# A diffusion-transformer layer on one core: 500 drawn plans for the list scheduler, and the last features' conditioning on TensorE

## The chip, the cores and the metric

One core of a Trainium2 chip runs the whole layer in one launch. The core has TensorE (matrix products into PSUM), VectorE, ScalarE and GpSimd, which work on SBUF and partly on PSUM, and a queue that issues DMAs (SyncE); ScalarE issues a few DMAs of its own. The profile calls them PE, DVE, ACT, POOL and SP; PEld is PE's weight load. The metric is the device time of one execution in microseconds, taken as the median of several runs.

## The reference

The layer takes latent tokens `x` (256 x 2048), context tokens `ctx` (256 x 2048) and two conditioning vectors, `c` for the latents and `c_ctx` for the context, all in float32. In short:

```python
sh1, sc1, g1, sh2, sc2, g2 = ada_mods(c, w_ada, b_ada)       # silu(c) @ w_ada + b_ada, w_ada is 2048 x 12288
csh1, csc1, *_ = ada_mods(c_ctx, w_ada, b_ada)
q, k, v = mixer_qkv(x * (1 + sc1) + sh1, w_in)               # w_in is 2048 x 3072; two head groups, rotary
qc, kc, vc = mixer_qkv(ctx * (1 + csc1) + csh1, w_in)        # keys and values of the context
heads = concat(window_attention(...), global_attention(...)) # latent queries on latent and context keys
x = layer_norm(2**0.25 * x + g1 * (heads @ w_out))           # w_out is 2048 x 2048
u = x * (1 + sc2) + sh2
x = layer_norm(2**0.25 * x + g2 * ((silu(u @ w_gate) * (u @ w_up)) @ w_down))   # hidden width 5632
```

With 256 + 256 tokens nearly every weight is read once, and the conditioning (`w_ada`) has as many bytes as two of the large weights.

## The kernel before, in words

**Arithmetic.** Products keep float32 accuracy by splitting both operands into a high part `hi` and a rest `lo` and adding three products of a faster type (`mm3`, lines 278 to 280, one line for each). ScalarE makes `hi` (a copy with a cast, line 519 in the planned part, 268 behind it), VectorE makes `lo` (a subtraction, lines 522 and 269). Every matmul of this kind has 128 x 128 weights and 512 moving columns.

**Features in groups.** The 16 blocks of 128 features (`k` 0 to 15) of `x` and `ctx` come in five groups: k 0; k 1; k 2 and 3; k 4 to 7; k 8 to 15 (`GROUPS`). For each group the kernel first needs shift and scale of these features. It loads the columns of `w_ada`, multiplies them with silu(c) and silu(c_ctx) (held as columns in `cs`), adds the bias (`shc`, `scc`), flips the tokens' features with TensorE (line 738), modulates them on ScalarE (744), splits them (`uh`, `ul`, lines 751 and 754), and multiplies them with the rows of `w_in` that belong to the group. A block of 512 columns of `w_in` is one "block"; four blocks hold queries (latents only, 2 row tiles), two hold keys and values (4 row tiles). The sums of a block live in SBUF (`qacc`, `kvacc`) from one group to the next.

**Two ways to sum the conditioning.** `flow_columns` does it on TensorE: four 32-column strips of the array take four k at a time (line 570, eight matmuls for a step of two 1 MB loads where four feature blocks are done together), ScalarE copies the bank (599), and TensorE adds the four strips and turns the row into columns with small products against `sel` (604). `flow_vector_columns` does it on VectorE: each load is multiplied by a scalar per partition and added to a running sum (632, 634), then the sum is turned and reduced (658, 661), and TensorE adds the partition groups with `fold` (685). The list `VECTOR_K` says which k take the second way: 12, that is the features k 12 to 15.

**Between groups.** From group index `SEED_G` on, a PSUM bank is first filled with the sums so far by ScalarE (`flow_seed`, line 534), the products are added on top, and ScalarE copies the bank back (803). Before that index the bank starts empty and VectorE adds it to the sums (805).

**What sets the order.** Everything up to the first feed-forward products is written as steps of a `Flow`: each has an engine, an assumed duration in ns, the steps that it follows, the buffers it takes and gives back, and an earliest time (`since`). `forward` runs a list schedule over five engines (SP stands for the DMA issue and the transfer's bandwidth): at each moment an engine starts, of its steps that are ready, the one with the lowest rank whose buffers are free. `backward` works out how late each step could start; these times become the ranks of the next round. `run` makes eight rounds, keeps the plan that ends first, and issues the instructions of each step in its order. The hardware queues then follow that order, each engine on its own, with semaphores between them: the assumed durations don't delay anything on the chip, they only decide the order.

The steps include 56 fillers (`WARM`, `warm_step`, matmul at line 1237 through `warm`), a chain of small matmuls on the identity. They depend only on each other and carry the highest first rank, so that the planner puts them where it sees nothing else for TensorE.

**After the plan.** A few first products of the feed-forward part are written by hand (lines 1549 to 1591), and the rest, some 740 us, is a plain program that the diff doesn't touch: `w_gate` and `w_up` products (`project`), the gate, a transposition through DRAM, `w_down`, and the second normalisation.

Of the kernel before, what the change touches and what calls it, by code (L numbers as in the profile page):

```python
# [47 lines left out]
VECTOR_K = (12,)  # L48
EARLY_WARM = 5
COLD = 3  # L50
SLACK = 2500
# [6 lines left out]
SEED_G = 3  # L58
# [16 lines left out]
class Flow:  # L75
# [8 lines left out]
    ROUNDS = 8  # L84

# [98 lines left out]

    def run(self):
        best, end = None, math.inf
        for _ in range(self.ROUNDS):
            order, last = self.forward()
            if not order:
                break  # L190
            if last < end:
                best, end = [(s, s.start, [b.pool for b in s.take]) for s in order], last
            late = self.backward(last)
            for i, s in enumerate(self.steps):
                s.rank = (late[s], i)
        assert best, "no step can start"
        for s, s.start, pools in best:
            for b, b.pool in zip(s.take, pools):
                pass
            s.fn()  # L200
# [3 lines left out]
def dit_layer(ctx: ExitStack, tc: tile.TileContext, x, c, cx, c_ctx, w_ada, b_ada, w_in, q_norm_g,  # L204
# [15 lines left out]
    def wk_bank():  # L220
        return wk_ps.tile([P, NB], F32, tag="wk", name="wk")
# [119 lines left out]
    fold = main.tile([P, 32], F32, tag="fold", name="fold")  # L341
    nc.vector.reduce_sum(fold, ident.rearrange("p (a i) -> p i a", a=4), axis=AX.X)
# [94 lines left out]
    def const_tables():  # L437
        nc.gpsimd.tensor_scalar_mul(nsink, sinkb, -1.0)
        for t in range(NT):
            for g, cg, sg in ((gq, cosQ, sinQ), (gk, cosK, sinK)):  # L440
# [19 lines left out]
             {"SP": 1300.0, "PE": 5600.0, "ACT": 5000.0, "DVE": 4000.0, "POOL": 4000.0})  # L460
# [68 lines left out]
    def flow_seed(ps, src, after):  # L529


        def fn():
            ps.t, ps.seeded = acc_bank(), True
            nc.scalar.copy(ps.t, src())

        return F.add("ACT", 475, fn, after, [ps])

    def flow_products(hl, deps, ready, cols, ps, xs, first, last, prev):
# [14 lines left out]
        return F.add("PE", 688 * len(cols), fn, after, [ps] if first and not seed else [], list(hl.rooms))  # L553
# [3 lines left out]
    def flow_columns(c0, ncol, shift, scale, ats, at):  # L557
# [18 lines left out]
        for g in range(ns):  # L576
            F.at = ats[g]
            ns1 = nk / 4 * (40 + 1.67 * width)
            if not c0:
                for i, k, m, since in ((0, 0, KD, 7200.0), (1, 0, KD // 2, 9700.0), (1, KD // 2, KD // 2, 11300.0)):  # L580
# [7 lines left out]
            if c0:  # L588
# [4 lines left out]
                prev = F.add("PE", 2 * ns1 + 420, both, [l0, l1, prev], [bank] if g == 0 else [], [r0, r1])  # L593
# [24 lines left out]
    def flow_vector_columns(c0, ncol, shift, scale, ats, at):  # L618

        width = ncol * P  # L620
        w = 2 * width
        nk = G4 * NB // w
        ns = KD // nk
        sums, last = [Buf("b4"), Buf("b4")], [None, None]

        def term(s, g, i, raw):
            if g == i == 0:
                sums[s].t = b4([P, 2 * NB], F32, "csum")
            a, src = sums[s].t[:, :w], raw.t[:, i * w : (i + 1) * w]
            k = 4 * (g * nk + i) + 2 + s  # L630
            if g == i == 0:
                nc.vector.tensor_scalar_mul(a, src, cs[:, k, None])
            else:
                nc.vector.scalar_tensor_tensor(a, src, cs[:, k, None], a, op0=ALU.mult, op1=ALU.add)  # L634

        for g in range(ns):
            F.at = ats[g * len(ats) // ns]
            raw = Buf("raw", "araw")

            def load(g=g, raw=raw):  # L640
                raw.t = pools[raw.pool].tile([P, G4 * NB], F32, tag="raw", name="raw")
                vector_load(raw.t, (c0, c0 + D), width, g)

            ld = F.add("SP", dma_ns(P * G4 * NB * 4, 2048), load, take=[raw])
            last_load[:] = [ld]
            for i in range(nk):
                for s in range(2):
                    last[s] = F.add("DVE", 1215, lambda s=s, g=g, i=i, raw=raw: term(s, g, i, raw), [ld, last[s]],
                                    [sums[s]] if g == i == 0 else [], [raw])
        F.at = at  # L650
        part = pa.tile([P, 2, w // 32], F32, tag="cpart", name="cpart")
        ready, ps = [], Buf("wk")
        for s in range(2):
            turned = Buf("b4")

            def turn(s=s, turned=turned):
                turned.t = b4([P, 2 * NB], F32, "cturn")[:, :w]
                nc.vector.transpose(turned.t, sums[s].t[:, :w])

            def reduce(s=s, turned=turned):  # L660
                nc.vector.reduce_sum(part[:, s, :], turned.t.rearrange("p (b j) -> p b j", j=32), axis=AX.X)

            a = F.add("DVE", 1150, turn, [last[s]], [turned], [sums[s]])
            ready.append(F.add("DVE", 1130, reduce, [a], give=[turned]))

        def gather():
            ps.t = wk_bank()
            fold_parts(ps.t, part, 2 * ncol)

        def add(i):  # L670
            pv = ps.t[:, : 4 * ncol].rearrange("p (s i j) -> p i j s", s=2, i=2)
            bs, bc = (bcol[:, k : k + ncol, None].to_broadcast([P, ncol, 2]) for k in (c0 // P, c0 // P + KD))
            if i == 0:
                nc.vector.tensor_tensor(shift, pv[:, 0], bs, op=ALU.add)
            else:
                nc.vector.scalar_tensor_tensor(scale, pv[:, 1], 1.0, bc, op0=ALU.add, op1=ALU.add)

# [1054 lines left out]
```

## Time and profile before

| | |
|---|---|
| median of 3 runs | 1137.29 us (1137.07 to 1138.73) |
| profiled execution | 1137.66 us, of which the trace spans 1135.9 |
| TensorE matmul busy | 1115.5 us, 98% |
| TensorE weight load busy | 904.2 us, 80% |
| VectorE busy | 858.8 us, 76% |
| ScalarE busy | 564.5 us, 50% |
| moved by DMA | 321.26 MB, mean 283 GB/s |
| mean granted TensorE clock | 0.995 |

How to read it: the share of busy time is a mean over stages with different limits. In about the first 140 us, when `w_ada` and the first half of `w_in` come in, the DMA engines are full. Between about 140 and 390 us (the last group, attention, the output projection) VectorE is nearly full. From about 390 us on the feed-forward products run. A matmul's row in the timeline has a start and a modelled end; neighbouring matmuls overlap in these rows, so the spacing of the starts says how long one takes, and a product of the split kind follows the one before after 0.23 us. A float32 matmul leaves two records. A wait shows as an idle time in brackets with the instruction that ended it.

### The profile page before, as it was taken

Reading aid. Unit: us, or ns where it says so; the run is one execution under the profiler, and the core shown is the slowest. Engines: PE = TensorE matmul, PEld = TensorE weight load, DVE = VectorE, ACT = ScalarE, POOL = GpSimd, SP = SyncE. Lnnn points to the kernel's source line nnn. Section 1 sums busy time; section 2 is a strip of 40 time slices with the busy share of each in tenths; the row PEclk is TensorE's granted clock in tenths of the full one; section 3 lists DMA queues with packets and bytes.
Section 4 is the critical chain, followed back from the end, with each engine's and each line's share of the span. In section 5 each row is a group of like instructions: output and inputs, shape, how many; then the busy total and the mean of one; then the engine's idle time right before and its main releaser. Section 6 shows DMA issues by size and latency. Waiting matters only on the chain.

```text
span 1135.9 us, 14202 instructions
## 1 busy us (share of the span) xinstructions
PE 1115.5 (98%) x5293; PEld 904.2 (80%) x5293; DVE 858.8 (76%) x1074; ACT 564.5 (50%) x815; POOL 40.1 (4%) x82
## 2 busy tenths in 40 slices
PE   8999999999999999999999999999999999999995
PEld 6766878777888788888888888888888888888884
DVE  4768999999998997767677566767766787676556
ACT  3444584977774355445464444454444443333341
POOL 1000040101100000000000000000000000000000
PEclk9999999999999999999999999999999999999998
DMA  9999999687999789999866776777777989877631
GB/s 299 384 384 396 382 353 371 217 299 227 348 340 388 280 296 316 321 313 319 302 204 211 251 223 224 244 246 249 221 245 246 306 315 333 318 274 253 203 137 74
DMA packets 186413, 321.26 MB, mean 283 GB/s; under 512 B 8764, under 2 KB 51164, under 8 KB 184039
## 3 DMA queue, kind: packets, MB, share of 16 engines
q1 hardware_dynamic: 184536, 319.25, 81.7%
q10 hardware_dynamic: 1808, 1.11, 0.3%
q8 instruction: 41, 0.67, 0.2%
q14 instruction: 28, 0.23, 0.1%
HBM read 304.07 MB, written 16.25 MB: 282 GB/s over the span
## 4 chain that ended last, share of the span: by engine, by line
PE 83%; DVE 7%; DMA 6%; ACT 1%; SPq 1%; issue 1%; DVEq 0%; ACTq 0%
PE acc L278 25%; PE acc L280 25%; PE acc L279 25%; DMA raw<-in_w_in_dram 4%; PE wk L1046 2%; DVE lo L522 2%; PE wk L570 1%; SPq L496 1%; DVE csum L634 1%; ACT hi L519 1%; PE wk L403 1%; DMA lgb<-in_ln_b_dram 1%; DVE hx L1028 1%; PE wk L738 0%; PE wk L1099 0%
## 5 line engine op out<-in xcount | busy, mean ns | idle before, releaser
L269 DVE TENSOR_TENSOR lo<-raw,hi 128x1024 fp32r<-128x1024 f32 x258 | 312.4, 1220 | 176.0 <-ACT hi L268 172.4
L268 ACT CAST hi<-raw 128x1024 fp32r<-128x1024 f32 x258 | 271.3, 1055 | 349.7 <-PE acc L280 298.5
L280 PE MATMUL acc<-hi,u2l 128*128 128x512 f32 x704 | 274.1, 389 | 1.2 <-DVE u2l L1556 1.2
L279 PE MATMUL acc<-lo,u2h 128*128 128x512 f32 x704 | 274.0, 389 | 0.6 <-DVE lo L269 0.6
L278 PE MATMUL acc<-hi,u2h 128*128 128x512 f32 x704 | 274.6, 390 | 0.0
L280 PEld LDWEIGHTS acc<-hi,u2l 128*128 128x128 f32 x704 | 132.1, 188 | 29.6 <-DVE u2l L1556 2.1
L279 PEld LDWEIGHTS acc<-lo,u2h 128*128 128x128 f32 x704 | 132.2, 188 | 28.1 <-DVE lo L269 1.0
L278 PEld LDWEIGHTS acc<-hi,u2h 128*128 128x128 f32 x704 | 132.2, 188 | 28.0 <-ACT u2h L1555 0.8
L519 ACT CAST hi<-raw 128x1024 fp32r<-128x1024 f32 (+1 forms) x86 | 87.7, 1032 | 97.7 <-PE acc L280 47.2
L278 PE MATMUL acc<-hi,hTh 128*128 128x512 f32 x344 | 135.5, 394 | 0.0
L280 PE MATMUL acc<-hi,hTl 128*128 128x512 f32 x344 | 133.9, 389 | 0.0
L279 PE MATMUL acc<-lo,hTh 128*128 128x512 f32 x344 | 133.9, 389 | 0.0
L393 DVE SCALAR_TENSOR_TENSOR adav<-raw,cs,adav 128x512 f32<-128x512 f32 (+1 forms) x128 | 121.2, 947 | 15.4 <-DMA raw<-in_w_ada_dram 13.6
L522 DVE TENSOR_TENSOR lo<-raw,hi 128x1024 fp32r<-128x1024 f32 (+1 forms) x86 | 101.3, 1194 | 18.8 <-ACT hi L519 18.7
L278 PE MATMUL acc<-hi,uh 128*128 128x512 f32 x256 | 103.5, 404 | 2.7 <-ACT qacc L803 2.6
L279 PE MATMUL acc<-lo,uh 128*128 128x512 f32 x256 | 100.1, 391 | 0.1
L280 PE MATMUL acc<-hi,ul 128*128 128x512 f32 x256 | 100.1, 391 | 0.0
L279 PEld LDWEIGHTS acc<-lo,hTh 128*128 128x128 f32 x344 | 64.6, 188 | 14.4 <-issue 0.7
L278 PEld LDWEIGHTS acc<-hi,hTh 128*128 128x128 f32 x344 | 64.6, 188 | 14.1 <-issue 1.0
L280 PEld LDWEIGHTS acc<-hi,hTl 128*128 128x128 f32 x344 | 64.6, 188 | 13.5
L278 PEld LDWEIGHTS acc<-hi,uh 128*128 128x128 f32 x256 | 48.1, 188 | 19.8 <-issue 4.6
L280 PEld LDWEIGHTS acc<-hi,ul 128*128 128x128 f32 x256 | 48.0, 188 | 10.8 <-DVE ul L754 0.4
(216 smaller groups left out, 1195.0 us busy)
## 6 DMA issues: line engine op xcount, KB each, us to landing
raw<-in_w_ada_dram SPq DMA_DIRECT2D x63, 1024.0 KB, 7.8
raw<-in_w_gate_dram SPq DMA_DIRECT2D x44, 1024.0 KB, 7.0
raw<-in_w_up_dram SPq DMA_DIRECT2D x44, 1024.0 KB, 5.4
raw<-in_w_down_dram SPq DMA_DIRECT2D x44, 1024.0 KB, 5.3
raw<-in_w_ada_dram SPq DMA_DIRECT2D x66, 512.0 KB, 6.4
raw<-in_w_in_dram SPq DMA_DIRECT2D x18, 1024.0 KB, 7.3
raw<-in_w_out_dram SPq DMA_DIRECT2D x16, 1024.0 KB, 9.3
pd<-hx SPq DMA_DIRECT2D x64, 128.0 KB, 3.9
```

The source lines that it names most:

```text
L268: nc.scalar.copy(hi[:, :n], raw[:, s : s + n])
L269: nc.vector.tensor_tensor(lo[:, :n], raw[:, s : s + n], hi[:, :n].bitcast(F32), op=ALU.subtract)
L278: nc.tensor.matmul(ps, lhsT=xh, rhs=w[0], start=first, stop=False, skip_group_check=seeded)
L279: nc.tensor.matmul(ps, lhsT=xh, rhs=w[1], start=False, stop=False, skip_group_check=seeded)
L280: nc.tensor.matmul(ps, lhsT=xl, rhs=w[0], start=False, stop=last, skip_group_check=seeded)
L393: nc.vector.scalar_tensor_tensor(a[:, c : c + piece], raw[:, f : f + piece], cs[:, 4 * (g * (G4 * NB // w) + j) + 2, None], a[:, c : c + p ...
L403: nc.tensor.matmul(ps, lhsT=ones, rhs=sb[:, s : s + NB], start=True, stop=True)
L496: nc.sync.dma_start(room.t.rearrange("p (k n) -> p k n", k=nk), w[k0 * P : (k0 + nk) * P, c0 : c0 + width].rearrange("(k p) n -> p k n", p=P),
L519: nc.scalar.copy(hl.hi[:, :n], raw.t[:, s : s + n])
L522: nc.vector.tensor_tensor(hl.lo[:, :n], raw.t[:, s : s + n], hl.hi[:, :n].bitcast(F32), op=ALU.subtract)
L570: nc.tensor.matmul(bank.t[32 * j : 32 * j + 32, :width], lhsT=cs[:, 4 * k + 2 - 2 * i : 4 * k + 34 - 2 * i], rhs=raw.t[:, c * width : (c + ...
L1046: nc.tensor.matmul(o_ps.t[:, : 2 * P].rearrange("p (g q) -> p g q", q=32), lhsT=v, rhs=pv[:, k], start=k == 0, stop=k == 3)
```

## The change

Four things are edited.

1. `run` keeps its eight rounds and then draws 500 variants: it takes the ranks of the best plan so far, changes those within a random stretch of time (each third one by a random amount, or all steps of one engine by the same amount), plans forward, and keeps the result if it ends earlier. After 3 in 10 of such finds it ranks all steps anew from the backward pass and plans once more. The generator has a fixed seed, so the order is the same in every build.
2. Durations and earliest times in the plan are set to other values, named in the diff. The loads of `x` and `ctx` get an earliest time by group (`X_FROM`), and where ScalarE issues them, a step with no instruction on SP stands for their bandwidth.
3. `VECTOR_K`, `flow_vector_columns`, `fold_parts` and the table `fold` are gone: k 12 to 15 take `flow_columns` too.
4. `SEED_G` goes from 3 to 4: only the last group (k 8 to 15) is seeded.

```diff
-VECTOR_K = (12,)
+X_FROM = {1: 13000.0, 2: 22000.0}
+CAST_FROM = 16300.0
+SEED = 7
-SEED_G = 3
+SEED_G = 4
+    TRIES = 500
...
+    def plan(self):
+        order, last = self.forward()
+        if order and last <= self.end:
+            self.end, self.rank = last, [s.rank[0] for s in self.steps]
+            self.best = [(s, s.start, [b.pool for b in s.take]) for s in order]
+            return True
+        return False
+
+    def give_ranks(self, ranks):
+        for i, (s, r) in enumerate(zip(self.steps, ranks)):
+            s.rank = (r, i)
+
+    def late_ranks(self, end):
+        late = self.backward(end)
+        self.give_ranks([late[s] for s in self.steps])
...
+        draw = random.Random(SEED)
+        for _ in range(self.TRIES):
+            ranks = list(self.rank)
+            a, w, d = draw.uniform(0, self.end), draw.uniform(2e3, 4e4), draw.gauss(0, 3e3)
+            near = [i for i, r in enumerate(ranks) if a <= r <= a + w]
+            kind, e = draw.random(), draw.choice(self.ENGINES)
+            for i in near:
+                if kind < 0.6:
+                    ranks[i] += draw.gauss(0, 3e3) if draw.random() < 0.3 else 0
+                else:
+                    ranks[i] += d if self.steps[i].eng == e else 0
+            self.give_ranks(ranks)
+            if self.plan() and draw.random() < 0.3:
+                self.late_ranks(self.end)
+                self.plan()
...
-    fold = main.tile([P, 32], F32, tag="fold", name="fold")
-    nc.vector.reduce_sum(fold, ident.rearrange("p (a i) -> p i a", a=4), axis=AX.X)
...
-             {"SP": 1300.0, "PE": 5600.0, "ACT": 5000.0, "DVE": 4000.0, "POOL": 4000.0})
+             {"SP": 2300.0, "PE": 5600.0, "ACT": 5000.0, "DVE": 4000.0, "POOL": 4000.0})
...
-        return F.add("ACT", 475, fn, after, [ps])
+        return F.add("ACT", 519, fn, after, [ps])
...
-        return F.add("PE", 688 * len(cols), fn, after, [ps] if first and not seed else [], list(hl.rooms))
+        return F.add("PE", 681 * len(cols), fn, after, [ps] if first and not seed else [], list(hl.rooms))
...
-                for i, k, m, since in ((0, 0, KD, 7200.0), (1, 0, KD // 2, 9700.0), (1, KD // 2, KD // 2, 11300.0)):
+                for i, k, m, since in ((0, 0, KD, 7200.0), (1, 0, KD // 2, 9900.0), (1, KD // 2, KD // 2, 11900.0)):
...
-                prev = F.add("PE", 2 * ns1 + 420, both, [l0, l1, prev], [bank] if g == 0 else [], [r0, r1])
+                prev = F.add("PE", 1865, both, [l0, l1, prev], [bank] if g == 0 else [], [r0, r1])
...
-    def flow_vector_columns(c0, ncol, shift, scale, ats, at):
...
-    def fold_parts(ps, part, n):
...
-        columns = flow_vector_columns if k0 in VECTOR_K else flow_columns
-        copy, ready = columns(k0 * P, n, shc[:, k0 : k0 + n, :], scc[:, k0 : k0 + n, :], ats, at + 0.8 * each)
+        copy, ready = flow_columns(k0 * P, n, shc[:, k0 : k0 + n, :], scc[:, k0 : k0 + n, :], ats, at + 0.8 * each)
...
-                a = F.add(issue, 500 if issue == "ACT" else max(ns, 500), load, take=room, since=9300.0)
-                loads.append((a, -4500) if issue == "ACT" else a)
+                a = F.add(issue, 500 if issue == "ACT" else max(ns, 500), load, take=room, since=X_FROM.get(k0, 0.0))
+                loads.append(F.add("SP", ns, lambda: None, [(a, -1000)]) if issue == "ACT" else a)
...
-                piece, = flow_weights(w_in, k0, 1, b0 * NB, m * NB, ("b4",), since=14000.0 if i and g == 0 else 0.0)
+                piece, = flow_weights(w_in, k0, 1, b0 * NB, m * NB, ("b4",), since=CAST_FROM if i and g == 0 else 0.0)
...
-            s = [F.add("PE", 760, lambda i=i, f=scores: f(i), qk, [banks[i]], [*qT[gi][0], *kT[w][0]]) for i in range(2)]
+            s = [F.add("PE", 745 if i else 690, lambda i=i, f=scores: f(i), qk, [banks[i]], [*qT[gi][0], *kT[w][0]]) for i in range(2)]
...
-            v = F.add("PE", 1760, values, g, [o_ps], [pT, *kv_room[w]])
+            v = F.add("PE", 1545, values, g, [o_ps], [pT, *kv_room[w]])
...
-                last = F.add("DVE", 1215, lambda g=g, i=i, room=room: vector_sum(room.t, a, w, g, i), [ld, last], give=[room])
+                last = F.add("DVE", 1197, lambda g=g, i=i, room=room: vector_sum(room.t, a, w, g, i), [ld, last], give=[room])
...
-            outs[n, t] = F.add("DVE", 710, spread, [(a, 80)])
+            outs[n, t] = F.add("DVE", 620, spread, [(a, 80)])
...
-            a = F.add("PE", 900, fn, [(last_sum, -SLACK)], [room])
+            a = F.add("PE", 860, fn, [(last_sum, -SLACK)], [room])
```

More of the change, by code (lines that the diff above doesn't have):

```diff
@@ L1 @@
 import heapq
+import random
 import math
@@ L183, in backward @@
         return start
+    def plan(self):
[11 more added lines that the diff above has]
+        self.give_ranks([late[s] for s in self.steps])
     def run(self):
-        best, end = None, math.inf
+        self.best, self.end = None, math.inf
         for _ in range(self.ROUNDS):
@@ L190, in run @@
                 break
[L191 to L197, printed above, removed]
+            self.plan()
+            self.late_ranks(last)
+        assert self.best, "no step can start"
+        draw = random.Random(SEED)
[12 more added lines that the diff above has]
+                self.late_ranks(self.end)
+                self.plan()
+        for s, s.start, pools in self.best:
             for b, b.pool in zip(s.take, pools):
@@ L616, in flow_columns @@
         return a, [F.add("DVE", 160, lambda i=i: add(i), [b, bias_ready], give=[ps]) for i in range(2)]
-    def flow_vector_columns(c0, ncol, shift, scale, ats, at):
[L620 to L676, printed above, removed]
-        b = F.add("PE", 500, gather, ready, [ps])
-        return b, [F.add("DVE", 160, lambda i=i: add(i), [b, bias_ready], give=[ps]) for i in range(2)]
@@ L681, in fold_parts @@
-    def fold_parts(ps, part, n):
-        pv = part.rearrange("p s (j r) -> p s j r", r=4)
-        for r in range(4):
-            nc.tensor.matmul(ps[32 * r : 32 * r + 32, : pv.shape[1] * n].rearrange("p (s j) -> p s j", j=n), lhsT=fold,
-                             rhs=pv[:, :, :, r], start=True, stop=True)
     u = {}
```

## The prediction

> **What bounds the kernel now.** I read the page first: busy shares, the slices, the chain of waits.
>
> ```profile
> span 1135.9 us, 14202 instructions
> ...
> PE 1115.5 (98%) x5293; PEld 904.2 (80%) x5293; DVE 858.8 (76%) x1074; ACT 564.5 (50%) x815; POOL 40.1 (4%) x82
> ...
> DVE  4768999999998997767677566767766787676556
> ...
> DMA  9999999687999789999866776777777989877631
> ...
> PE 83%; DVE 7%; DMA 6%; ACT 1%; SPq 1%; issue 1%; DVEq 0%; ACTq 0%
> ```
>
> TensorE (PE) holds the chain. VectorE (DVE) is full from slice 6 to slice 13, about 140 to 370 us, and the DMA engines are full up to about 140 us. So the first question is whether TensorE loses anything to either there. Next the windows by stage, with TensorE's matmul records and weight loads counted:
>
> ```profile
> 28.40:145.00 116.60, 116.35 (x724) 84.15 (x722) 94.22 (x110) 56.25 (x89) 0.00 (x0) 1.00 1.05 383
> 145.00:392.00 247.00, 245.59 (x1145) 196.65 (x1145) 232.79 (x366) 165.43 (x326) 27.39 (x58) 1.00 0.90 312
> ...
> 700.00:800.00 100.00, 100.00 (x443) 82.81 (x442) 72.04 (x86) 48.47 (x55) 0.00 (x0) 1.00 0.73 238
> ```
>
> The columns are length, then busy time (and records) of PE, PEld, DVE, ACT, POOL, then clock, DMA share, GB/s. In the feed-forward stage 443 matmuls take 100 us, 226 ns each, without a gap. Busy time could still hide waits, since the ends of matmuls are modelled, so I went to starts. Two waits stand out in the list of waits of PE, and the timeline shows them and the smaller ones as starts that come later than 0.23 us after the one before:
>
> ```profile
> PE acc L278 <- ACT qacc L803: 2.6, 1, 2.6
> ...
> PE acc L280 <- DVE u2l L1556: 1.2, 1, 1.2
> ```
>
> ```profile
> 5.47 2.50 PE L1237 MATMUL wk<-ident 128*128 128x128 f32 x10
> ...
> 14.51 2.70 PE L1237 MATMUL wk<-ident 128*128 128x128 f32 x22
> 16.97 0.48 PE L278 MATMUL acc<-hi,uh 128*128 128x512 f32 x1
> ...
> 25.05 0.39 PE L280 MATMUL acc<-hi,ul 128*128 128x512 f32 x1
> 28.05 0.50 PE L278 MATMUL acc<-hi,uh 128*128 128x512 f32 x1 [2.61 <-ACT qacc L803]
> ...
> 74.95 0.40 PE L280 MATMUL acc<-hi,ul 128*128 128x512 f32 x1
> 75.48 1.06 PE L604 MATMUL wk<-sel,ada 128*128 128x4 f32 x8
> ...
> 118.64 4.62 PE L1237 MATMUL wk<-ident 128*128 128x128 f32 x40
> 123.02 0.48 PE L278 MATMUL acc<-hi,uh 128*128 128x512 f32 x1
> ...
> 264.07 0.40 PE L280 MATMUL acc<-hi,oTl 128*128 128x512 f32 x1
> 264.54 1.99 PE L1046 MATMUL wk<-pT,kvacc 128*128 128x256 f32 x8
> ...
> 390.25 0.40 PE L279 MATMUL acc<-lo,u2h 128*128 128x512 f32 x1
> 391.85 0.50 PE L280 MATMUL acc<-hi,u2l 128*128 128x512 f32 x1 [1.20 <-DVE u2l L1556]
> ```
>
> From 25.05 to 28.05 are 3.00 us where 0.23 is normal: 2.8 lost. At 75 us 0.3 is lost, at 264 us 0.24, and four more starts of this kind between 138 and 149 us, where DVE has the least room, add some 0.9: 1.4 in all for the six. With the 1.4 at 390 us (1.60 from start to start, less 0.23; the list counts from the modelled end), everything that TensorE waits for between its first product at 16.97 us and the end of the planned part is **about 5.6 us**. Between 145 and 392 us a full DVE costs TensorE almost nothing.
>
> Then there are the fillers, L1237: matmuls of the identity that the plan issues when it sees nothing else for TensorE, two records each.
>
> ```profile
> L1237 PE MATMUL wk<-ident 128*128 128x128 f32 x112 | 15.8, 293 | 0.0
> ```
>
> 112 records are 56 fillers, the constant WARM. The twenty at 118.64 us hold TensorE for 4.4 us (to 123.02), 0.22 each. The point on which my forecast rests: each filler is a step of the plan like any other, the plan is complete only with all its steps, and the diff leaves WARM at 56. A better order moves fillers; it doesn't remove them. So TensorE's time to the end of the planned part is the sum of real work, 56 fillers and true waits, and only the first and the last can change.
>
> **The change part by part.** *The last features (k 12 to 15).* DVE loses:
>
> ```profile
> L634 DVE SCALAR_TENSOR_TENSOR csum<-raw,cs,csum 128x1024 f32<-128x1024 f32 x30 | 36.4, 1273 | 0.5 <-DMA raw<-in_w_ada_dram 0.5
> ...
> L658 DVE STREAM_TRANSPOSE cturn<-csum 128x1024 f32<-128x1024 f32 x2 | 2.4, 1213 | 0.0
> ...
> L661 DVE TENSOR_REDUCE cpart<-cturn 128x32 f32<-128x1024 f32 x2 | 2.3, 1202 | 0.0
> ```
>
> 36.4 + 2.4 + 2.3 = 41.1 us, and two first products (L632) beside these. TensorE gains what flow_columns issues: four steps of eight matmuls (16 records, two loads of 1 MB each), then four small sums. The trace has both for k 8 to 11, and the fold that goes:
>
> ```profile
> 110.85 0.39 PE L280 MATMUL acc<-hi,ul 128*128 128x512 f32 x1
> 111.17 1.92 PE L570 MATMUL wk<-raw,cs 128*32 128x512 f32 x16
> 113.02 0.50 PE L278 MATMUL acc<-hi,uh 128*128 128x512 f32 x1
> 113.36 0.40 PE L279 MATMUL acc<-lo,uh 128*128 128x512 f32 x1
> ...
> 132.00 0.95 PE L604 MATMUL wk<-sel,ada 128*128 128x4 f32 x8
> 132.80 1.07 PE L738 MATMUL wk<-ident,xt 128*128 128x128 f32 x8
> ...
> 145.15 0.26 PE L685 MATMUL wk<-cpart,fold 128*32 128x16 f32 x8
> 145.52 0.50 PE L278 MATMUL acc<-hi,uh 128*128 128x512 f32 x1
> ```
>
> One step between products: 110.85 to 113.36 is 2.51, less two normal spacings of 0.23, 2.05. Four are 8.2; if they stand side by side the changes to and fro are saved, 4 x 1.85 + 0.2 = 7.6. The sums take 132.80 - 132.00 = 0.8, the fold gave back 0.4. Added to TensorE: **8.0 to 8.6; I take 8.6**, since the plan kept such steps apart for k 8 to 11. One ACT copy of the bank (0.6, by L534's copy of the same size below) joins the queue ahead of the modulation; SP issues 8 loads of 1 MB instead of 16 of 512 KB, the same bytes, and they return their rooms after two matmul steps rather than after DVE's queue.
>
> In its sentence apart: the Trainium skill, "Perfetto Trace Analysis", Identifying the Most-Contended Engine, says that matmul busy time is a poor measure and that headroom is read from the share of weight loads. By it PEld's 80% would leave a fifth free and the 8.6 would cost nothing. The 700 to 800 row stands against it: 82.81 of 100 with 443 matmuls at an even 226 ns, so the missing 17% is spacing, not room.
>
> *Seeds of group 3 (k 4 to 7).* Sixteen banks are no longer filled by ACT ahead of the products, and their sums leave by an addition on DVE instead of a copy on ACT.
>
> ```profile
> L534 ACT COPY acc<-qacc 128x512 f32<-128x512 f32 x16 | 9.2, 587 | 0.2
> ...
> L805 DVE TENSOR_TENSOR qacc<-qacc,acc 128x512 f32<-128x512 f32 x16 | 10.7, 682 | 3.6 <-PE acc L280 3.6
> ```
>
> ACT sheds 32 x 0.59 = 19 us, DVE takes 16 x 0.68 = 11; with the above DVE is still 30 us lighter. TensorE's work is the same. If DVE comes late with such an addition, a bank returns late; by the row above that is some tenths of a us, and I take zero, up to 1 kept for the range.
>
> *The planner.* The 500 draws run on the host. They, the new durations and earliest times (X_FROM, CAST_FROM, SP from 2300) change only the order, the issue of x and ctx included: for k 1 and k 2 to 3 these (0.26 + 0.52 MB; at 383 GB/s 2 us of DMA) now stand later in ACT's queue, behind casts, and no longer ahead of the weights whose landing ends the 2.8 us wait. They wait there behind whatever cast or copy stands first; what waits for them are the flips of k 1 and k 2 (k 3 with it), TensorE's products behind those. So the most that all reordering can give is the 5.6 us of waits, and where it fills them it does so with fillers taken from 118 us. I expect back the 2.8 and the 0.9 at 138 to 149 us, where DVE's sums are gone: 3.7 of the 5.6. The u2l wait comes of the order after the plan, which stays. Bounds: 5.6 regained, or nothing regained and new waits.
>
> New waits have no row in this trace. From below zero; from above each is worth the one at 25 us, 2.8, and I allow two of them at the most, with DMA at 1.05 and each step now wanting two whole loads. I take 0.5 (nearer to zero, since in the 364 us after 28 us there are only small ones and the one at 390).
>
> *Sum* against the profiled execution, 1137.66 (1135.9 span + 1.76 around it): + 8.6 - 3.7 + 0.5 = + 5.4, so 1143.1. This execution is 0.37 above the median of the runs, 1137.29, so in their terms **1142.7**.
>
> **The rivals.**
>
> *All waits go.* + 8.6 - 5.6 = + 3.0: 1140.3. For it: a search that keeps the earliest of 500 plans, with times from a trace. Against it: the plan's time is not the chip's; at 118 us it placed 4.4 us of fillers where nothing waits after.
>
> *Not slower, by fewer changes between kinds of matmul.* The first L278 after another kind starts its successor late (113.02 to 113.36 is 0.34, not 0.23), and this is in the group means:
>
> ```profile
> L278 PE MATMUL acc<-hi,uh 128*128 128x512 f32 x256 | 103.5, 404 | 2.7 <-ACT qacc L803 2.6
> L279 PE MATMUL acc<-lo,uh 128*128 128x512 f32 x256 | 100.1, 391 | 0.1
> ```
>
> 256 x 13 ns = 3.3 us, and each column step pays a further 0.1 before it. An order that halves the changes gives 1.7 to 2.0, and steps side by side lower the 8.6 to 8.0. With all waits gone: 8.0 - 5.6 - 2.0 = + 0.4, 1137.7: no change. It decides only if both happen nearly in full. To be faster, it needs work that I don't see in the diff to leave TensorE, or the fillers to cost nothing.
>
> *New waits.* The order chosen is the one that the model flatters most, and the twenty fillers that gave DMA and DVE time at 118 us now stand earlier. Two new waits of 2.8 with 2.8 of the old regained and the rest kept: 8.6 - 2.8 + 5.6 = + 11.4, 1148.7. Against it: TensorE has more of its own work before 145 us, so it is the data that get more time. In its sentence apart: the Trainium skill, "TensorE: Matmul & The Clock Gate", Part 1, says that an idle window of about 3.4 us halves the clock until a busy one has passed; a wait of that length would cost a further 1.7, an estimate from that page. The trace agrees at the start (five fillers take 2.50 at 5.47 us, eleven take 2.70 at 14.51), but the 2.8 at 25 us slowed nothing.
>
> *The draws find no better plan*, and TensorE merely gets 8.6 more with no wait regained: 1145.9. It lies within the forecast's spread.
>
> **How the numbers follow.** Forecast with its spread (1140.8 to 1147) 0.56; all waits gone, 1139.7 to 1140.8, 0.14; not slower by fewer changes 0.12; new waits (over 1147) 0.12; faster for a reason not seen here 0.06. What tells from no change is 0.2%, 2.3 us: slower means above 1139.6, faster below 1135.0. Slower 0.56 + 0.14 + 0.12 = 0.82, less 0.04 for the edge of the second case: 0.78; same 0.12 + 0.04 = 0.16; faster 0.06. The range runs from 1138.0, inside the not-slower case, to 1149.0, inside the new waits, and leaves out about 0.2; it takes in both ends of every cost above.
>
> **What would show it.** L570 with 384 records instead of 320, L604 with 32, L634, L658, L661 and L685 gone, L534 16 fewer and L805 16 more; L1237 still 112 records, now nearly all before 60 us; no wait of over 1 us at 25 us; DVE's busy time in 28 to 145 us down by over 25 us, and in 145 to 392 us little changed; the feed-forward stage the same in rate, merely later by the total. Wrong would be: fewer than 112 filler records, a wait list of PE longer than two entries beyond the start, or a first product much off 16.97 us. If the kernel is faster with TensorE's records as counted, then spacing that I took for fixed was waiting.

## The result, and the profile after

The changed kernel takes 1144.51 us (median of 4 runs, 1144.07 to 1145.23); the kernel before took 1137.18 beside it. The ratio is 1.0059 with a 95% interval of 1.0044 to 1.0074: slower by about 7 us, where 5.4 was forecast; the time lies inside the stated range. The profiled execution took 1144.55 us, of which the trace spans 1142.8, against 1135.9 before: 6.9 us to explain.

First the page after: the span, the busy shares, the slices of VectorE, the chain by engine. Lines have moved with the diff: the three products are L310 to L312 (L278 to L280 before), the column sums L600 (L570), the fillers L1196 (L1237).

```profile
span 1142.8 us, 14235 instructions
...
PE 1123.8 (98%) x5357; PEld 907.7 (79%) x5357; DVE 828.3 (72%) x1053; ACT 548.3 (48%) x784; POOL 45.8 (4%) x82
...
DVE  3764479899999897767667566766766787676556
...
PE 96%; DVE 2%; ACT 0%; DMA 0%; issue 0%; POOL 0%; DVEq 0%; ACTq 0%; POOLq 0%
```

TensorE has 64 records more (5357 for 5293: 64 column sums and 8 small ones more, 8 folds less), VectorE is 30.5 us less busy, and the chain, which was 83% TensorE, is now 96% TensorE: the change took nearly everything else off the path and lengthened the path itself. The windows by stage of the changed kernel (columns as in the prediction):

```profile
28.40:145.00 116.60, 116.60 (x732) 79.34 (x734) 66.28 (x96) 42.42 (x64) 0.00 (x0) 1.00 0.99 358
145.00:392.00 247.00, 247.00 (x1156) 201.09 (x1152) 227.29 (x356) 161.07 (x314) 31.17 (x57) 1.00 0.91 315
...
700.00:800.00 100.00, 100.00 (x443) 82.81 (x442) 69.92 (x81) 48.36 (x57) 0.00 (x0) 1.00 0.74 246
```

VectorE's 94.2 us between 28 and 145 us became 66.3. The DMA rate there fell from 383 to 358 GB/s. The feed-forward stage is the same, 443 matmuls in 100 us. So the time lies before it. Where, the timeline of TensorE says (starts and lengths; the first product is at 21.88 us, the first feed-forward product at 397.08):

```profile
6.23 5.06 PE L1196 MATMUL wk<-ident 128*128 128x128 f32 x22
...
19.95 2.17 PE L1196 MATMUL wk<-ident 128*128 128x128 f32 x18
21.88 0.48 PE L310 MATMUL acc<-hi,uh 128*128 128x512 f32 x1
...
209.37 1.33 PE L1196 MATMUL wk<-ident 128*128 128x128 f32 x10
...
397.08 0.50 PE L310 MATMUL acc<-hi,u2h 128*128 128x512 f32 x1 [1.42 <-ACT u2h L1514]
```

Before, these two starts were at 16.97 and 389.92. So 4.9 us were lost before the first product, 2.25 between the first product and the feed-forward part (375.20 for 372.95), and a net 0.3 came back behind. The last two figures are cut at a wait: the 1.42 us at 397.08 count in the 2.25, while the kernel before has its wait of 1.20 behind that mark, at 391.85. Right behind it 1.4 us come back, and about 1.1 are lost again in small pieces of the feed-forward part. Before the first product stand 43 fillers where 28 stood, and the plan put 13 more behind it, eleven of them between 209 and 246 us, in the middle of attention. The records by line, and TensorE's list of waits:

```profile
L310 PE MATMUL acc<-hi,uh 128*128 128x512 f32 x256 | 104.8, 409 | 0.0
...
L600 PE MATMUL wk<-raw,cs 128*32 128x512 f32 x192 | 23.1, 598 | 0.0
...
L1196 PE MATMUL wk<-ident 128*128 128x128 f32 x112 | 17.5, 308 | 0.0
...
L600 PE MATMUL wk<-raw,cs 128*32 128x128 f32 x128 | 4.6, 286 | 0.0
...
L634 PE MATMUL wk<-sel,ada 128*128 128x4 f32 x32 | 3.9, 237 | 0.0
...
L600 PE MATMUL wk<-raw,cs 128*32 128x256 f32 x64 | 3.9, 382 | 0.0
```

```profile
PE wk L361 <- DMA crow<-in_c_ctx_dram: 2.1, 1, 2.1
PE wk L359 <- POOL ident masks.py:199: 1.5, 1, 1.5
PE acc L310 <- ACT u2h L1514: 1.4, 1, 1.4
PE acc L311 <- DVE lo L301: 0.8, 1, 0.8
PE wk L1366 <- DVE xt L1131: 0.3, 1, 0.3
```

Still 112 filler records, and 384 of the column sums (192 + 128 + 64). The wait at 25 us and the small ones are gone; one at the first feed-forward product stays (on ScalarE's `u2h` now, 1.4, where it was VectorE's `u2l`, 1.2). Added up start to start over the planned part, the column sums take 7.0 us more, the small sums 0.7 more, the fold 0.4 less: 7.35 us of new work. The waits behind the first product fell by 4.2, from 5.6 to 1.4. What ate that: 0.8 on the wait for `crow` at the very start, 0.8 because more fillers ran in the first microseconds, where a filler takes 0.5 us, and some 1.3 on more changes between kinds of matmul (TensorE changes into products 78 times for 65, and the mean of the first of three products rose from 404 to 409 ns over 256 of them). This makes 6.05 of the 6.9 us; the other 0.85 is spread over places of some tenths each.

### The profile page after: what moved, and what is told of

Its sections match the earlier page's. It is cut to its first block, busy times and chain, and to the rows that moved or that the text cites. A ratio compares the mean times of both kernels' runs of the same rounds, so it can differ in the third digit from the quotient of the medians.

```text
span 1142.8 us, 14235 instructions
## 1 busy us (share of the span) xinstructions
PE 1123.8 (98%) x5357; PEld 907.7 (79%) x5357; DVE 828.3 (72%) x1053; ACT 548.3 (48%) x784; POOL 45.8 (4%) x82
## 4 chain that ended last, share of the span: by engine, by line
PE 96%; DVE 2%; ACT 0%; DMA 0%; issue 0%; POOL 0%; DVEq 0%; ACTq 0%; POOLq 0%
PE acc L310 28%; PE acc L311 28%; PE acc L312 28%; PE wk L600 3%; PE wk L1005 2%; PE wk L1196 1%; PE wk L310 1%; PE wk L312 1%; PE wk L697 1%; PE wk L311 1%; PE wk L433 1%; PE wk L1058 0%; DMA crow<-in_c_ctx_dram 0%; DVE xt L1600 0%; DVE xt L1596 0%; PE wk L1333 0%
## 5 line engine op out<-in xcount | busy, mean ns | idle before, releaser
L310 PE MATMUL acc<-hi,u2h 128*128 128x512 f32 x704 | 274.7, 390 | 1.4 <-ACT u2h L1514 1.4
L312 PE MATMUL acc<-hi,u2l 128*128 128x512 f32 x704 | 274.1, 389 | 0.0
L310 PEld LDWEIGHTS acc<-hi,u2h 128*128 128x128 f32 x704 | 132.2, 188 | 29.9 <-ACT u2h L1514 2.3
L311 PEld LDWEIGHTS acc<-lo,u2h 128*128 128x128 f32 x704 | 132.2, 188 | 28.4 <-DVE lo L301 1.1
L312 PEld LDWEIGHTS acc<-hi,u2l 128*128 128x128 f32 x704 | 132.1, 188 | 27.8 <-DVE u2l L1515 0.6
L310 PE MATMUL acc<-hi,hTh 128*128 128x512 f32 x344 | 135.5, 394 | 0.0
L312 PE MATMUL acc<-hi,hTl 128*128 128x512 f32 x344 | 133.9, 389 | 0.0
L310 PE MATMUL acc<-hi,uh 128*128 128x512 f32 x256 | 104.8, 409 | 0.0
L312 PE MATMUL acc<-hi,ul 128*128 128x512 f32 x256 | 100.1, 391 | 0.0
L310 PEld LDWEIGHTS acc<-hi,hTh 128*128 128x128 f32 x344 | 64.6, 188 | 14.3 <-issue 1.0
L312 PEld LDWEIGHTS acc<-hi,hTl 128*128 128x128 f32 x344 | 64.6, 188 | 13.6
L310 PEld LDWEIGHTS acc<-hi,uh 128*128 128x128 f32 x256 | 48.2, 188 | 18.4 <-issue 8.2
L312 PEld LDWEIGHTS acc<-hi,ul 128*128 128x128 f32 x256 | 48.1, 188 | 10.7
```

Of the source, the lines that this page charges most:

```text
L310: nc.tensor.matmul(ps, lhsT=xh, rhs=w[0], start=first, stop=False, skip_group_check=seeded)
L311: nc.tensor.matmul(ps, lhsT=xh, rhs=w[1], start=False, stop=False, skip_group_check=seeded)
L312: nc.tensor.matmul(ps, lhsT=xl, rhs=w[0], start=False, stop=last, skip_group_check=seeded)
```

## The experiments

Every ratio is against runs of the kernel before on the same chip, with its 95% interval. "VectorE's sums" are the sums of k 12 to 15 as they were before the change.

**1. VectorE's sums put back into the changed kernel.**

```diff
+VECTOR_K = (12,)
...
-        copy, ready = flow_columns(k0 * P, n, shc[:, k0 : k0 + n, :], scc[:, k0 : k0 + n, :], ats, at + 0.8 * each)
+        columns = flow_vector_columns if k0 in VECTOR_K else flow_columns
+        copy, ready = columns(k0 * P, n, shc[:, k0 : k0 + n, :], scc[:, k0 : k0 + n, :], ats, at + 0.8 * each)
```

(with `flow_vector_columns`, `fold_parts` and `fold` as they were)

> The changed kernel with one part undone: the features k 12 to 15 are again summed on VectorE (flow_vector_columns, fold), everything else (draws, durations, SEED_G 4) as changed. Theory A (TensorE is the bound: its time is real work, 56 fillers and true waits, and the column sums brought 7.4 us of work): 7 us less than the changed kernel, 1136 to 1139, about the kernel before. Rival B (the draws and the later first product, 21.9 us instead of 17.0, made it slow, and TensorE's extra work is hidden): stays at 1142 or above. Either way L570's successor shows 320 records and TensorE's waits beyond the start stay below 6 us under A.

Measured: 1158.93 us, ratio 1.0179 (1.0165 to 1.0193). A fails. The number lies in B's range, but B would have left the time about where it was, and this is 14 us slower than the changed kernel with 7.4 us less work on TensorE: neither theory has the cause. TensorE's list of waits in this run (total us, count, longest):

```profile
PE wk L771 <- issue: 11.9, 1, 11.9
PE acc L311 <- DVE qacc L838: 3.7, 1, 3.7
```

The longest in TensorE's timeline (start, length; the wait before it in brackets):

```profile
149.88 1.09 PE L771 MATMUL wk<-ident,cxt 128*128 128x128 f32 x4 [11.87 <-issue]
```

VectorE's timeline over the same time:

```profile
124.73 16.82 DVE L667 SCALAR_TENSOR_TENSOR csum<-raw,cs,csum 128x1024 f32<-128x1024 f32 x14
141.47 0.16 DVE L643 TENSOR_TENSOR shc<-wk,bcol 128x8 f32<-128x8 f32 x1
...
149.62 0.16 DVE L645 SCALAR_TENSOR_TENSOR scc<-wk,bcol 128x8 f32<-128x8 f32 x1
```

And the window of 30 us around it, columns as in the stage windows:

```profile
120.00:150.00 30.00, 15.06 (x69) 10.81 (x70) 30.00 (x31) 5.25 (x7) 0.00 (x0) 0.76 1.05 395
```

VectorE is busy for all of the 30 us. The two small additions that finish shift and scale of k 8 to 11 (L643 and L645, 0.16 us each) stand in its queue behind 14 sums of 1.2 us and then behind the turning and reducing; the second runs at 149.62, and the next moment ScalarE modulates and TensorE's flip goes on after 11.9 us of waiting. TensorE worked half of the window and its granted clock was 0.76 over it. So the order can lose far more than the 5.6 us of waits that it could win, and here the place is VectorE's queue.

**2. The same without the draws.** The edit of 1, and `TRIES = 0`.

> The changed kernel with VectorE's sums of k 12 to 15 put back and without the draws. Rival H (VectorE's queue meets any order but that of before): 1145 or above, waits of several us on VectorE or on flips between 100 and 160 us. Rival G (the 500 draws chose the bad order of the first of these runs): about 1137 to 1140.

Measured: 1170.97, ratio 1.0289 (1.0275 to 1.0304): H holds, and G, that the draws chose the bad order, falls; with VectorE's sums the draws gained 12 us. Its waits:

```profile
PE wk L718 <- DVE cpart L694: 17.5, 1, 17.5
PE acc L312 <- DVE lo L555: 4.6, 1, 4.6
PE acc L311 <- DVE kvacc L838: 4.0, 1, 4.0
```

TensorE's fold waited 17.5 us for VectorE's reduced sums.

**3. VectorE's sums and SEED_G 3 in the changed kernel.** The edit of 1, and `SEED_G = 3`.

> The changed kernel with VectorE's sums put back (as in the first of these runs, 1158.9) and SEED_G back to 3, new durations and draws kept. Theory L (group 3's additions, 11 us more of VectorE's work just where its sums run, made its queue late): 1138 to 1146, longest wait on VectorE or on flips under 5 us. Rival M (the new durations make the order that VectorE can't keep): 1150 or above.

Measured: 1150.9, ratio 1.0102 (1.0082 to 1.0121). The number is in M's range. Taking group 3's additions off VectorE, which is another order too, brings back some 8 of the 21 us by which run 1 is over the kernel before; 13 remain. But the longest wait is one on a load of `x`, not on VectorE:

```profile
PE wk L771 <- DMA xt<-in_x_dram: 5.4, 1, 5.4
```

Against the trace before, the first product comes 3.0 us later (1.2 of it the landing of `crow`), the part from there to the feed-forward products is 8.0 longer, with this wait and a granted clock of 0.50 from 134.9 to 141.6 us, and 2.2 are lost after that. Which of the new durations or earliest times makes this order was not separated.

**4. SEED_G 3 in the changed kernel**, sums on TensorE.

> The changed kernel with SEED_G back to 3 (k 4 to 7 seeded by ScalarE), sums on TensorE, durations and draws as changed. Theory A (TensorE's work is the same either way and VectorE has room): 1144.5 within 2 us. Theory L's counterpart (the additions on VectorE cost even here): 1142 or below.

Measured: 1145.64, ratio 1.0059 (1.0040 to 1.0078), as the changed kernel's own. With the sums gone from VectorE the additions cost nothing there, as predicted.

**5. The column sums alone, in the kernel before.**

```diff
-VECTOR_K = (12,)
+VECTOR_K = ()
```

> The kernel before with one part of the change alone: VECTOR_K empty, so k 12 to 15 are summed on TensorE, with the eight old rounds, the old durations and SEED_G 3. Theory A: slower than before by the added 7.4 us of TensorE work less what the order regains of 5.6 us of waits: 1141 to 1146. Rival C (VectorE, full from 140 to 370 us, was the bound, and relief there pays for the work): 1137 or below.

Measured: 1148.97, ratio 1.0098 (1.0084 to 1.0112), 11 us over before; above A's bounds, and against C. Relief on VectorE alone brought nothing that shows. Beside the 7.4 us of work there are new waits where the other order met VectorE after all (the two on `kTl`; the one on `crow` is a landing at the start):

```profile
PE wk L329 <- DMA crow<-in_c_ctx_dram: 2.5, 1, 2.5
PE wk L949 <- DVE kTl L911: 1.6, 1, 1.6
...
PE wk L902 <- DVE kTl L911: 1.1, 1, 1.1
```

These waits don't make up all of the difference; the rest is in small pieces that were not followed up. Draws, durations and SEED_G together are worth some 4 us to the kernel with column sums (1148.97 to 1144.51, two chips, each by its ratio: 1.0098 to 1.0059).

**6. The draws left out of the changed kernel.**

```diff
-    TRIES = 500
+    TRIES = 0
```

> The changed kernel without the 500 draws (TRIES 0, the eight rounds alone). Theory A (the order can only move waits and the changes between kinds of matmul): within 3 us of the changed kernel, 1142 to 1148, TensorE's records the same. Rival F (the draws win much and only hide how dear the rest is): 1150 or above. Rival G (the draws chose a worse order than the rounds): 1141 or below.

Measured: 1146.8, ratio 1.0075 (1.0062 to 1.0087): A holds. The draws gain some 2 us here by the medians, but this interval and the changed kernel's (1.0044 to 1.0074) overlap, so a gain isn't shown.

**7. The draws alone, in the kernel before** (old durations, VectorE's sums, SEED_G 3; `run` and its helpers as changed).

> The kernel before with the 500 draws alone (old durations, VectorE's sums, SEED_G 3). Theory A (the order moves only waits): 1135 to 1140. Rival H (any other order with VectorE's sums meets VectorE's queue): 1142 or above. Rival J (the draws are good and the new durations are what spoils the order): 1135 or below.

Measured: 1143.15, ratio 1.0047 (1.0035 to 1.0060): 5.4 us slower for a plan that the scheduler held to be no later. The number is H's: the order of the kernel before, which the eight rounds gave, is better on the chip than its model knows. But the loss isn't where H has it. Between 145 and 392 us TensorE is busy for 245.45 us, as before (245.59), and the part from the first product to the feed-forward part is only 0.8 us longer. The first product comes 2.1 later (1.3 of it the landing of `crow`), and 2.6 are lost behind the first feed-forward product:

```profile
399.91 1.09 PE L1438 MATMUL wk<-ident,xt 128*128 128x128 f32 x4 [2.69 <-DVE xt L1203]
...
401.65 0.63 PE L311 MATMUL acc<-hi,u2l 128*128 128x512 f32 x1
402.08 0.63 PE L309 MATMUL acc<-hi,u2h 128*128 128x512 f32 x1
```

VectorE's queue is in it after all: four sums of 0.75 us stand there between the short steps of the normalisation that this `xt` waits for, and in the kernel before they stand behind them. After the wait products follow at 0.43 us until 403 us (granted clock 0.50 from 399.8 to 403.1).

**8. Another seed in the changed kernel.**

```diff
-SEED = 7
+SEED = 8
```

> The changed kernel with another seed for the draws (8 instead of 7). Theory A: with the sums on TensorE no order waits much, so 1144.5 within 2.5 us. Rival K (the time of the changed kernel is the luck of one draw): off by more than 4 us to either side.

Measured: 1144.65, ratio 1.0060 (1.0046 to 1.0073), the same as with seed 7. With the sums on TensorE two draws ended alike: A.

**9. Twenty fillers fewer in the changed kernel's plan.**

```diff
-WARM = 56
+WARM = 36
```

> The changed kernel with one number changed: 36 fillers instead of 56. Theory A (a filler beyond the true waits costs its 0.22 us): 20 x 0.22 = 4.4 us less, about 1140, down to 2 us less if waits take the place of some. Rival D (the fillers only cover time in which TensorE waits for the first columns and weights anyway): 1144.5, unchanged, with about 4 us of waits in their place. Rival E (without them the clock falls to half after a wait): slower than 1144.5, and fillers or products at 0.4 us spacing beyond the first 12 us.

Measured: 1140.99, ratio 1.0024 (1.0014 to 1.0033): about 4 us less than the changed kernel's 1.0059, and A's 4.4 nearly whole. The first product comes at 18.23 instead of 21.88 us. This is another order as well, with 32 of the 36 fillers ahead of the first product; run 12 keeps the order.

**10. The same in the kernel before** (`WARM = 36`).

> The kernel before with 36 fillers instead of 56, the sums of k 12 to 15 on VectorE as before. Theory A (every filler beyond the true waits costs 0.22 us): 4.4 us less than before, about 1133. Rival H (the kernel before owes its time to one fortunate order of VectorE's queue; with other fillers the eight rounds give another order, and TensorE waits on VectorE as it did in the run with VectorE's sums put back): 1140 or above, with waits of several us on VectorE between 100 and 160 us.

Measured: 1141.35, ratio 1.0035 (1.0021 to 1.0048): slower. A's 1133 is refuted here, and the number is H's, though H's waits of several us on VectorE aren't there. The trace of TensorE shows smaller things:

```profile
28.10 0.50 PE L278 MATMUL acc<-hi,uh 128*128 128x512 f32 x1 [2.68 <-ACT qacc L803]
...
29.43 0.63 PE L280 MATMUL acc<-hi,ul 128*128 128x512 f32 x1
29.86 0.63 PE L278 MATMUL acc<-hi,uh 128*128 128x512 f32 x1
...
128.24 0.80 PE L279 MATMUL acc<-lo,uh 128*128 128x512 f32 x1 [1.61 <-DVE lo L522]
128.83 0.63 PE L280 MATMUL acc<-hi,ul 128*128 128x512 f32 x1
129.26 0.63 PE L278 MATMUL acc<-hi,uh 128*128 128x512 f32 x1
```

Between 125 and 141 us TensorE waits three times (0.7, 1.6 and 1.0 us), and twice its products follow at 0.43 us instead of 0.23 for some 3.3 us, from 29.4 and from 128.2 us (granted clock 0.50 in both stretches). The first of these stands behind the same wait at 25 us that slowed nothing in the kernel before: 2.68 us here, 2.61 there. But this is also another order, so the next run kept the order.

**11. The kernel before in its very order, its last twenty fillers not issued.**

```diff
-        warm(wps.t, 1)
+        if i < 36:
+            warm(wps.t, 1)
```

> The kernel before in its very order, planned with 56 fillers, but the last 20 of them, which stood at 118.6 us, are not issued. Theory A (they hold TensorE for 4.4 us in which nothing is waited for, since a block of weights was ready): 1133, TensorE's waits as before. Rival D (they gave VectorE and the loads time that is needed anyway): 1136.5 to 1137.5, with some 4 us of new waits on VectorE or on loads right behind 118 us or up to 150 us.

Measured: 1139.19 beside 1138.16, ratio 1.0002 (0.9989 to 1.0016): no change. D holds, by way of a load, and my reading of the fillers at 118 us is wrong. The timeline of TensorE in this run, with the wait in brackets:

```profile
123.66 0.39 PE L280 MATMUL acc<-hi,ul 128*128 128x512 f32 x1
123.98 1.07 PE L570 MATMUL wk<-raw,cs 128*32 128x512 f32 x8
128.59 1.06 PE L570 MATMUL wk<-raw,cs 128*32 128x512 f32 x8 [3.55 <-DMA raw<-in_w_ada_dram]
129.59 0.50 PE L278 MATMUL acc<-hi,uh 128*128 128x512 f32 x1
...
131.08 0.63 PE L279 MATMUL acc<-lo,uh 128*128 128x512 f32 x1
131.50 0.63 PE L280 MATMUL acc<-hi,ul 128*128 128x512 f32 x1
```

The window around it:

```profile
120.00:150.00 30.00, 26.45 (x130) 20.47 (x129) 29.33 (x30) 17.89 (x29) 5.36 (x8) 0.89 1.04 376
```

The block behind the fillers was indeed ready and ran 4.4 us earlier. But the next column step then reached TensorE at 123.98, found the first of its two loads, and waited 3.55 us for the second, until 128.59; in the kernel before the same step starts at 128.65 and finds both. The fillers at 118 us covered a landing 10 us later. And the wait was long enough to cost the clock: the products behind it follow at 0.42 us (131.08 to 131.50) until about 136 us, and the granted clock of the window is 0.89. Step for step against the trace before, this run is 4.6 us ahead at 118 us, 0.9 ahead after the wait, and 2.3 behind at 137 us, when the rate is back: the slow stretch cost 3.3 us, twice the prediction's estimate of 1.7. The Trainium skill, "TensorE: Matmul & The Clock Gate", Part 1, gives about 3.4 us of idle time for this. A wait of 3.55 us agrees with it, but as a limit below which a wait is harmless it doesn't hold here: in runs 3, 7 and 10 the rate halved after waits of 2.44, 2.69 and 2.68 us (2.8 to 3.1 from start to start), and the measurement decides.

**12. The changed kernel in its very order, only its first twenty fillers issued** (as in run 11, with `i < 20`).

> The changed kernel in its very order, but only the first 20 of its 56 fillers are issued: 23 fewer ahead of the first product at 21.9 us, 13 fewer behind it. Theory A at its fullest (none of them covers a wait): 36 x 0.22 = 7.9 us less, 1136.6. Rival D (those ahead of the first product cover the landing of the first columns and weights; only the 13 later ones cost): 2.9 us less, 1141.6, with waits of about 5 us before the first product. Rival E (the clock falls for lack of work early on): 1143 or above, and products spaced over 0.4 us near 20 us.

Measured: 1140.37 beside 1138.16, ratio 1.0013 (1.0002 to 1.0024): some 5 us less than the changed kernel, between A's 7.9 and D's 2.9. The timeline around the first product:

```profile
15.88 0.39 PE L634 MATMUL wk<-sel,ada 128*128 128x4 f32 x2 [0.39 <-ACT ada L629]
16.13 0.42 PE L697 MATMUL wk<-ident,xt 128*128 128x128 f32 x2
18.05 0.50 PE L310 MATMUL acc<-hi,uh 128*128 128x512 f32 x1 [1.50 <-ACT uh L710]
```

The first product starts at 18.05, 3.8 us earlier, with 1.9 us of waits before it: so most of the 23 fillers that the plan had put there (5 us) only delayed it. Behind the first product the planned part is 1.9 us shorter (373.27 for 375.20), less than 13 x 0.22 = 2.9. E falls: the products behind the first follow at 0.23 us. No version that was run beats the kernel before.

## Why the prediction was right, and where it was not

**That TensorE's time is work, fillers and waits: right in sign and as bookkeeping.** The trace after has the records that were listed (384 column sums, 32 small ones, 112 fillers), 7.35 us of new work where 8.6 was taken: the steps themselves came at 1.85 us as costed; part of the change to and fro that I had put into them appeared instead in the products, which is the 1.3 us above. The wait at 25 us and the small ones went, the one at the first feed-forward product stayed, all as said. Of the prediction's three signs of being wrong two came all the same: the first product is far off 16.97 us, and the list of waits has three entries beyond the start (1.4, 0.8 and 0.3 us). The records were right; where the fillers would stand was not.

**The size: + 7.3 for + 5.4.** In the terms of the sum, the 8.6 came out (7.35 and 1.3), and 4.2 were regained for 3.7. The term that was too small is the 0.5 for what is new: in its place stand 2.45 us, 0.8 for `crow`, 0.8 for fillers at the slow rate of the start and 0.85 in small pieces. The sum had nothing for a later first product. It came 4.9 us later: 0.8 of this is `crow`, and the rest is mostly fillers, 43 instead of 28, more of them in the first microseconds, where each takes twice as long. Most of it came back behind the first product, since 15 fillers (3.3 us) fewer stand there. I wrote that the fillers would stand nearly all before 60 us and that the first product would stay at 16.97; 45 of the 56 stood before 60 us, and the first product moved.

**How much of it was luck.** The four other plans with the sums on TensorE and all 56 fillers (runs 4, 5, 6 and 8) took between 1.0059 and 1.0098 of the time before, up to 4.4 us over the changed kernel; run 5 lies above the forecast's spread. The sum had no means to say which order the planner would find.

**"Nothing waits after" the fillers at 118 us: wrong.** Run 11 shows a load behind them. The prediction looked at the next block and its weights and not at the step after, whose load is what TensorE would have met. So in the kernel before, 20 of the 56 fillers were free, and at that one step TensorE is held to the pace of the DMA queues (1.05 busy between 28 and 145 us). The sum stays true as an account of one trace, but it doesn't say that taking a filler away shortens it. In the changed kernel the fillers do cost: runs 9 and 12 gained about 4 and 5 us.

**"The most that reordering can give is 5.6" was argued as a bound on one side; on the other side I allowed 5.6 of new waits.** That was far too little for orders with VectorE's sums: runs 1, 2 and 3 lost 13 to 33 us. The rival of new waits named DMA as its place; runs 1 and 2 put the longest on VectorE's queue, run 3 on a load. For the changed kernel itself the rival didn't come; run 1, which only puts those sums back, has it.

**"Between 145 and 392 us a full VectorE costs TensorE almost nothing": true, but not the whole of it.** It held for the order of run 7 too. But VectorE is full from about 114 us on (28.22 of 28.4 us between 113.6 and 142 us in the trace before), and not from 140 as I read the slices, and the long waits of runs 1 and 2 stand between 119 and 165 us. So the relief of VectorE is worth something after all: with the new durations, SEED_G 4 and the draws it is worth 14 us net of the 7.4 us of work (1158.93 against 1144.51). Against the kernel before, whose order happened to avoid such waits, there was nothing to win.

**The other rivals.** All waits gone: they nearly went, but the start moved. Not slower by fewer changes between kinds: the changes became more. The draws find no better plan: not settled; run 6 puts them at about 2 us, and the intervals overlap. A longer idle time halving the rate: the prediction took the wait at 25 us as harmless because nothing slowed behind it; run 10 shows that a wait of the same length there can be followed by half the rate.

**What stays open.** No run adds the column sums to an order that is otherwise unchanged, so the 7.35 us of work rest on the traces' starts alone. Which of the new durations or earliest times spoils the order with VectorE's sums (run 3 leaves 13 us after SEED_G is undone), and how much of the 4.9 us at the start comes from the earliest times and how much from the forced fillers; run 12 says that fillers are the larger part.

## What to carry to other kernels

When one engine is busy throughout, an account of its time by kind, start to start, gives the sign of a change that adds work to it; but a piece of idle or filler time is free or dear by the first wait that would take its place, and that is looked for several steps ahead in the engine's queue, loads included. A planner that improves its own estimate need not improve the chip's time, since its queues are fixed in order and it can't know when a load is late: small steps that others wait for (here additions of 0.16 us) should not be queued behind long ones that are needed later. Fillers of a fixed number are work like any other once there is less to cover.

## What the runs showed of the hardware that was not expected

- The first landing of the run varies from one execution to the next with nothing changed in front of it: TensorE waited for `crow` 1.3 us in the trace before, 2.6 us in run 11, which has the same order there, and 2.1 us in the changed kernel. That much of a difference between two single traces is no effect of a change.
- A wait of 3.55 us (run 11) was followed by half of TensorE's rate for about 7 us (0.42 us from product to product, granted clock 0.50 from 130.1 to 136.8 us). Shorter waits went either way: after 2.61 us at 25 us the kernel before stayed at 0.23, while after 2.68 us at the same place (run 10), 2.69 us at 397 us (run 7) and 2.44 us at 405 us (run 3) products followed at 0.43 us for some 3 us, with a granted clock of 0.50. So a wait of 2.4 to 2.7 us isn't safe, and one trace without a loss doesn't make it so.
